# A decoder layer's projections: TensorE in program order, gates deferred, x in natural order, bias repeats pinned, value stores merged

## The chip, the cores and the metric

The kernel runs on one core of a Trainium2 chip, in one launch. The metric is the device time of that launch in microseconds; lower is better. The engines are TensorE (PE, with its weight loads as PEld), VectorE (DVE), ScalarE (ACT), GpSimd (POOL) and SyncE (SP), which mostly issues transfers. ACT issues transfers too; "SPq" and "ACTq" in the profile are the two sequencers at that work.

## What is computed

One layer of a causal decoder on x of 2048 tokens by 1024 columns, all in float32:

```python
nx   = rmsnorm(h, attn_norm_g)
proj = nx @ w_in          # 1024 x 3088: gq gk gv gr glow dq dk dv
glog = log_sigmoid(glow @ gla_gate_w2 + gla_gate_b) / 16
o_a  = gla_mixer(gq, gk, gv, glog)   # chunked gated linear attention, 4 heads
o_a  = rmsnorm_per_head(o_a) * gla_norm_g * silu(gr)
o_b  = dilated_mixer(dq, dk, dv, rel_bias)  # 8 heads, 3 dilations 1, 4, 16
h    = h + concat(o_a, o_b) @ w_out
h    = h + square(relu(rmsnorm(h) @ w_ff1)) @ w_ff2
y    = rmsnorm(h)
```

The change touches the first stage alone: the norm of x, its transposes, the product with `w_in`, the gate, and the rows of biases that the dilated attention reads later.

## The kernel before

Every product in float32 precision is made of three (`mm3`, L66 to L69): the operands are split into a high part (ACT, `split` L345 for x, `prep` L202 for weights) and a rest (DVE, L346, L204, L206). On top of that the projections save an eighth of the products by a block scheme with seven products for eight (`order = (1, 2, 5, 6, 3, 4, 7)`): tokens are halved into tiles 0 to 3 and 4 to 7 (a half of the sequence is eight tiles of 128), the contraction is halved, and the columns of a group are halved.

The work is a list of 126 jobs: two halves of the sequence, nine column groups (`dv gr dq dk dq dk gq gk gv`) and seven products each. `prep(at + 2)` makes the weights of the job after next; `product(at, i)` runs PE and returns `rest`, which combines the result on DVE, ACT and POOL (L302 to L321) and calls `finish` where a block is complete. Jobs of 256 or 264 columns have four products, one for each tile; jobs of 128 columns have one. `finish` stores what is done. For `gr` (jobs 7 to 13 and 70 to 76) it makes silu by way of `log_sigmoid` (L125 to L128: Abs, Exp, Ln on ACT, one operation on DVE), another Exp (L260) and two multiplications (L261, L262), and the last 16 columns, `glow`, go to `gate` (L222 to L233): a transpose on PE (L227), a copy on DVE (L228), a product (L230), `log_sigmoid` and a store. Both PE results lie in PSUM banks with the tag "d", of which there are two. The job that completes `gr` does so for two tiles at a time (blocks 21 and 22), so eight gates arise in its four products.

x of the first half of the sequence is loaded, normed and transposed in the block ahead of the loop (`x_load`, `x_stat`, `x_scale`, `first_half`). That block is a manual schedule: PE, DVE, ACT and POOL take their instructions in program order. x of the second half goes through a generator, `second_half`, one step at each job listed in `OTHER` (7, 9, 10, 11, 12, then 14, 18, 21, 22, 23 and so on every 14): load, norm, two steps of transposes (L378), sums and stores to `nTD`. `reload` brings these back for the second half. Tokens are permuted in all transposed tiles: `token_rows` has partition 8r + i hold token 16i + r, so that 16 tokens of one residue lie side by side.

Behind the first block (jobs 5 and on) nothing is in program order: a scheduler, which times each instruction with a model of its own, orders what every engine issues, PE too. Where the real times differ, an engine waits in the order that was fixed.

`bias_rows` (job 65) computes a row of biases for each head and dilation and stores it to `rowD`; `spread_bias` (L338 to L342), called at every third job from 71 on, has ACT issue a transfer that repeats such rows over 128 partitions into `rbD`, for two heads at a time, twelve times in all.

Of the kernel before, what the change touches and what calls it, by code (L numbers as in the profile page):

```python
# [18 lines left out]
D = 1024  # L19
# [22 lines left out]
def emit(tc, a, stop=99):  # L42
# [34 lines left out]
    ident = const.tile([128, 128], F32, name="ident")  # L77
    make_identity(nc, ident)
    mhalf = const.tile([128, 4], F32, name="mhalf")
    V.memset(mhalf, -0.5)  # L80
    stats = const.tile([128, 96], F32, name="stats")
    stat_at = [0]

    def stat(n=1):
        if stat_at[0] + n > 96:
            stat_at[0] = 0
        s = stats[:, stat_at[0]:stat_at[0] + n]
        stat_at[0] += n
        return s
# [132 lines left out]
    def gate(glow, t):  # L222

        gT = gTs[t % 2]
        V.memset(gT, 1.0)
        pt = ps("d")
        T.transpose(pt[:16, :128], glow, ident)  # L227
        V.tensor_copy(gT[:16], pt[:16, :128])  # L228
        pg = ps("d")[:, :256]
        T.matmul(pg, gT, w2b, start=True, stop=True)  # L230
        e = stage()[:, :256]
        log_sigmoid(e, pg)
        SP.dma_start(glD[t * 128:t * 128 + 128], e)  # L233

    def finish(g, n, k, i):
# [32 lines left out]
        q = SP if g == 0 else A  # L268
        q.dma_start((vD if kind == "dv" else gvD)[tk, j:j + w], s)
        if kind == "dv":  # L270
            q.dma_start(token_rows(vN[:, j:], t, 512, w), s)

    banks = [0]

    def product(at, i):
# [7 lines left out]
        if w == 128:  # L283
            n = 512
            for c in range(4):
                mm3(p, W[0][:, c], W[1][:, c], B[0][:, c], B[1][:, c], c == 0, c == 3)
        else:
            p = p[:, :w]
            tk = slice(i * 128, i * 128 + 128)
            for c in range(4):  # L290
                mm3(p, B[0][:, c, tk], B[1][:, c, tk], W[0][:, c], W[1][:, c], c == 0, c == 3)

        def rest():
# [31 lines left out]
    def bias_rows():  # L325
# [4 lines left out]
        V.tensor_scalar(rb[:32], rb[:32], -1.0, None, op0=OP.mult)  # L330
        SP.dma_start(oh, a["c_onehot"])
        for d in range(3):
            p = ps("o")
# [4 lines left out]
    def spread_bias(d, h):  # L338

        row = rowD[h:, d]  # L340
        A.dma_start(rbD[d][h:h + 2].rearrange("h p n -> p h n"),
                    bass.AP(tensor=row.tensor, offset=row.offset, ap=[[0, 128], [3 * 384, 2], [1, 384]]))  # L342

# [4 lines left out]
    def x_load(t, dst):  # L348
        SP.dma_start(dst, token_rows(x2, t, D))

# [20 lines left out]

    def transposed(xt, last=None):
        out = []
        for q in range(2):
            pv = view(ps("cd"[q]), (4, 128))
            for k in range(4):
                of = xt[:, (4 * q + k) * 128:(4 * q + k + 1) * 128]
                T.transpose(pv[:, k, :], last if last is not None and 4 * q + k == 7 else of, ident)  # L378
            out.append(pv)
# [5 lines left out]
    def first_half(t):  # L385

        pv = transposed(xs[t])
        i = t % 4
# [21 lines left out]
    def second_half():  # L410

        b = [view(bp[:, 512 * q:], (4, 128)) for q in range(4)]
        for i in range(4):
# [10 lines left out]
            for k in range(2):  # L424
                for q, pv in enumerate(transposed(xp[:, D * k:])):
                    A.activation(b[2 * k + q], pv, AF.Copy)
# [15 lines left out]
    with tc.manual_schedule(engines={nc.tensor.engine, nc.vector.engine, nc.scalar.engine, nc.gpsimd.engine}):  # L442
        x_load(0, xs[0])
        SP.dma_start(gB, bcast_row(a["attn_norm_g"], D))
        load_w(0, 0, 0)
# [53 lines left out]
    prep(6)  # L499
    other, back = second_half(), []  # L500
    for at in range(5, len(jobs)):
        g = jobs[at][0]
# [10 lines left out]
        if at in OTHER:  # L513
            next(other)
        if at == 7 * NG + 2:
            bias_rows()
        if 7 * NG + 8 <= at < 7 * NG + 44 and at % 3 == 0:
            spread_bias(2 - (at - 7 * NG - 8) // 12, (at - 7 * NG - 8) // 3 % 4 * 2)
    if stop <= 1:
        es.close()  # L520
# [871 lines left out]
```

## Time and profile before

| | |
|---|---|
| median of 3 runs | 2400.09 us (2397.44 to 2403.56) |
| the profiled execution | 2398.99 us, span 2397.2 us |
| mean granted TensorE clock | 0.985 |
| PE busy | 2306.6 us (96%) |
| DVE, ACT, POOL busy | 1561.9, 1148.0, 583.3 us (65%, 48%, 24%) |
| chain that ended last | PE 77%, DMA 8%, DVE 7%, issue 3%, ACT 3% |
| DMA | 458.13 MB, mean 191 GB/s |

The projections take the first 582 us, the attentions go on to about 960 us, and the rest is the output projection and the MLP. PE is busy almost throughout, but its matmuls are pipelined and their ends are modelled, so the times at which it stood idle tell more than the share. A "granted clock" below 1.00 means that for part of the stretch PE ran at half speed. A wait line reads: who waited, for whom, us in total, times, longest.

### The profile page before, as it was taken

The page shows a single profiled execution, that of the slowest core. Times are in us where ns is not written, and L with a number is a line of the kernel's source. Part 1 is how long each engine was busy: PE and PEld are TensorE (multiplying, and loading weights), DVE is VectorE, ACT ScalarE, POOL GpSimd, SP SyncE. Part 2 cuts the span into 40 slices and gives each one's busy share as a digit, 9 for nine tenths or more (in the row PEclk, how much of TensorE's full clock was granted, in tenths as well). Part 3 has the DMA queues.
Part 4 walks back from the last instruction along what each step waited for, and adds up shares of the span by engine and source line. Part 5 has one row for each costly group of instructions (what it writes and reads, how often), then busy time and mean ns, then how long its engine had stood idle before and what let it go on. Part 6 is the DMA issues. An engine that isn't in the chain of part 4 may idle for free.

```text
span 2397.2 us, 35124 instructions
## 1 busy us (share of the span) xinstructions
PE 2306.6 (96%) x12648; PEld 1989.9 (83%) x12648; DVE 1561.9 (65%) x2879; ACT 1148.0 (48%) x2181; POOL 583.3 (24%) x551
## 2 busy tenths in 40 slices
PE   6999998999999989999999999999999999999998
PEld 5877898779989988888788887888888888888886
DVE  6878666765667668445677778877773455556555
ACT  5565434533767657223455556555563333224323
POOL 5555435446566665100000000000000100001002
PEclk9999999999999999999999999999999999999999
DMA  6457664757888867468664447544467496457653
GB/s 159 120 164 230 213 189 136 206 166 194 213 193 226 225 174 241 154 201 267 203 206 145 145 149 242 176 162 157 155 203 274 155 315 208 168 170 248 217 167 106
DMA packets 342540, 458.13 MB, mean 191 GB/s; under 512 B 19620, under 2 KB 215733, under 8 KB 336094
## 3 DMA queue, kind: packets, MB, share of 16 engines
q1 hardware_dynamic: 313614, 413.15, 56.0%
q10 hardware_dynamic: 28752, 42.74, 5.2%
q8 instruction: 99, 1.62, 0.3%
q14 instruction: 75, 0.61, 0.1%
HBM read 293.51 MB, written 167.02 MB: 192 GB/s over the span
## 4 chain that ended last, share of the span: by engine, by line
PE 77%; DMA 8%; DVE 7%; issue 3%; ACT 3%; POOL 1%; SPq 1%; ACTq 0%; POOLq 0%; DVEq 0%
PE ps_a L67 8%; PE ps_a L68 8%; PE ps_a L69 8%; PE ps_c L67 7%; PE ps_c L69 7%; PE ps_c L68 7%; PE ps_d L67 4%; PE ps_d L69 4%; PE ps_d L68 4%; PE ps_a L672 4%; PE ps_o L67 3%; PE ps_o L68 3%; PE ps_o L69 3%; PE ps_d L653 2%; DMA cmb<-boD 2%
## 5 line engine op out<-in xcount | busy, mean ns | idle before, releaser
L1226 POOL TENSOR_TENSOR suma<-suma,gs 128x512 f32<-128x512 f32 x16 | 23.3, 1472 | 1152.6 <-ACT scr L1224 1152.5
L346 DVE TENSOR_TENSOR ca<-ra,ca 128x1024 fp32r<-128x1024 f32 x112 | 137.7, 1230 | 164.4 <-ACT ca L345 164.4
L345 ACT ACTIVATE ca<-ra 128x1024 fp32r<-128x1024 f32 x112 | 118.0, 1054 | 225.8 <-PE ps_c L69 185.4
L345 ACT ACTIVATE w1comb<-w1raw 128x512 fp32r<-128x512 f32 x224 | 139.6, 627 | 158.7 <-PE ps_c L69 57.7
L644 ACT ACTIVATE pe<-pe,O 128x256 f32<-128x256 f32 (+1 forms) x384 | 157.6, 454 | 89.1 <-DVE O L643 76.3
L672 PE MATMUL ps_a<-v,pt 128*128 128x65 f32 x1200 | 185.1, 258 | 13.3 <-DVE pt L662 8.5
L672 PEld LDWEIGHTS ps_a<-v,pt 128*128 128x128 f32 x1200 | 180.9, 200 | 16.1 <-DVE pt L662 9.5
L346 DVE TENSOR_TENSOR w1comb<-w1raw,w1comb 128x512 fp32r<-128x512 f32 x224 | 153.6, 689 | 53.4 <-ACT w1comb L345 53.2
L653 PE MATMUL ps_d<-ident,pe 128*128 128x128 f32 x600 | 160.9, 284 | 0.0
L643 DVE CUSTOM_DVE_ANT_0 pe<-ps_c,nb 128x256 f32<-128x256 f32 (+1 forms) x384 | 126.6, 360 | 43.4 <-PE ps_d L653 20.6
L204 DVE TENSOR_TENSOR wcomb<-wraw,wcomb 128x512 fp32r<-128x512 f32 (+2 forms) x84 | 101.2, 1210 | 70.3 <-ACT wcomb L202 68.8
L202 ACT ACTIVATE wcomb<-wraw 128x512 fp32r<-128x512 f32 (+2 forms) x126 | 96.3, 773 | 103.7 <-PE ps_a L69 20.8
L345 ACT ACTIVATE cb<-rb 128x1024 fp32r<-128x1024 f32 x56 | 59.4, 1061 | 158.0 <-PE ps_o L68 108.1
L67 PE MATMUL ps_c<-hb,w1comb 128*128 128x512 f32 x336 | 132.2, 393 | 2.8 <-ACT hb L345 2.8
L68 PE MATMUL ps_c<-hb,w1comb 128*128 128x512 f32 x336 | 132.2, 393 | 1.6 <-DVE w1comb L346 1.6
L69 PE MATMUL ps_c<-hb,w1comb 128*128 128x512 f32 x336 | 131.8, 392 | 0.0
L67 PE MATMUL ps_c<-cb,ca 128*128 128x512 f32 x336 | 130.8, 389 | 0.0
L68 PE MATMUL ps_c<-cb,ca 128*128 128x512 f32 x336 | 130.8, 389 | 0.0
L69 PE MATMUL ps_c<-cb,ca 128*128 128x512 f32 x336 | 130.8, 389 | 0.0
L653 PEld LDWEIGHTS ps_d<-ident,pe 128*128 128x128 f32 x600 | 111.1, 190 | 0.4
L94 POOL TENSOR_TENSOR stats<-stats,mhalf 128x1 f32<-128x1 f32 (+1 forms) x64 | 46.4, 730 | 259.3 <-DVE stats L93 216.1
L346 DVE TENSOR_TENSOR cb<-rb,cb 128x1024 fp32r<-128x1024 f32 x56 | 68.2, 1221 | 62.5 <-ACT cb L345 62.3
(351 smaller groups left out, 7330.2 us busy)
## 6 DMA issues: line engine op xcount, KB each, us to landing
ra<-actD SPq DMA_DIRECT2D x56, 1024.0 KB, 6.8
actD<-acc SPq DMA_DIRECT2D x192, 256.0 KB, 2.3
rb<-w_ff SPq DMA_DIRECT2D x72, 512.0 KB, 4.8
w1raw<-w_ff SPq DMA_DIRECT2D x32, 1024.0 KB, 7.3
k<-kD SPq DMA_DIRECT2D x32, 512.0 KB, 11.5
rb<-hTD SPq DMA_DIRECT2D x14, 1024.0 KB, 5.9
wraw<-w_in SPq DMA_DIRECT2D x48, 256.0 KB, 3.4
boD<-O SPq DMA_DIRECT2D x8, 1056.0 KB, 6.2
```

Of the source, the lines that this page charges most:

```text
L67: T.matmul(out, sh, mh, start=first, stop=False)
L68: T.matmul(out, sl, mh, start=False, stop=False)
L69: T.matmul(out, sh, ml, start=False, stop=last)
L94: G.tensor_tensor(r2, r, mhalf[:, :n], op=OP.pow)
L202: A.activation(hi, src, AF.Copy, scale=sc)
L204: V.tensor_tensor(lo, src, hi.bitcast(F32), op=OP.subtract)
L345: A.activation(hi, src, AF.Copy)
L346: V.tensor_tensor(lo, src, hi.bitcast(F32), op=OP.subtract)
L643: V.tensor_tensor_reduce(p, s, bias, scale=1.0, scalar=BIG, op0=OP.add, op1=OP.min, accum_out=nm)
L644: A.activation(p, p, AF.Exp, bias=nm, scale=-1.0)
L653: T.transpose(pb[:, i * 128:i * 128 + 128], src, ident)
L672: T.matmul(self.b.opsum[:, n % 4], self.pt[:, i * 128:i * 128 + 128], self.b.v[:, blk, cols], start=first, stop=last)
```

## The change

Six edits:

- The loop over jobs 5 to 125 is put under a manual schedule for TensorE alone: PE's instructions keep program order, those of the other engines are still ordered by the scheduler.
- `gate` is cut in two. Its transpose is put in a list `waiting` that the next `product` empties behind its own matmuls; the transpose puts the gate's product in the list for the product after that. The two buffers `gTs` alternate by block of four tiles in place of by tile.
- `x_load` reads 128 consecutive tokens in natural order. The permutation goes into the transposes: they take a matrix `perm` in place of `ident` (made on POOL at the start). The ring of statistics is cut from 96 to 48 columns.
- The gain `gB` is no longer loaded with a transfer that repeats its row over 128 partitions: one row is loaded by ACT's queue and spread by two products with a row of ones, which ACT copies out of PSUM. ACT does both copies ahead of its first statistic of x.
- Values (`dv`, `gv`) are stored to `vD` and `gvD` once for four tiles; the stores of `vN` stay one for each tile.
- `bias_rows` is begun at job 63 (loads) and continued at job 66 (products); each transfer of `spread_bias` is pinned behind what ACT was given before it in the program.

```diff
--- before.py
+++ after.py
@@ -76,13 +76,18 @@
     A.preload_act_table_set("natural_log_exp_and_others")
     ident = const.tile([128, 128], F32, name="ident")
     make_identity(nc, ident)
+
+    perm = const.tile([128, 128], F32, name="perm")
+    G.memset(perm, 0.0)
+    G.affine_select(out=perm, in_=perm, compare_op=OP.not_equal, fill=1.0, base=0, pattern=[[-1, 16], [-16, 8]],
+                    channel_multiplier=1)
     mhalf = const.tile([128, 4], F32, name="mhalf")
     V.memset(mhalf, -0.5)
-    stats = const.tile([128, 96], F32, name="stats")
+    stats = const.tile([128, 48], F32, name="stats")
     stat_at = [0]
 
     def stat(n=1):
-        if stat_at[0] + n > 96:
+        if stat_at[0] + n > 48:
             stat_at[0] = 0
         s = stats[:, stat_at[0]:stat_at[0] + n]
         stat_at[0] += n
@@ -221,16 +226,23 @@
 
     def gate(glow, t):
 
-        gT = gTs[t % 2]
-        V.memset(gT, 1.0)
-        pt = ps("d")
-        T.transpose(pt[:16, :128], glow, ident)
-        V.tensor_copy(gT[:16], pt[:16, :128])
-        pg = ps("d")[:, :256]
-        T.matmul(pg, gT, w2b, start=True, stop=True)
-        e = stage()[:, :256]
-        log_sigmoid(e, pg)
-        SP.dma_start(glD[t * 128:t * 128 + 128], e)
+        gT = gTs[t // 4 % 2]
+
+        def transpose():
+            V.memset(gT, 1.0)
+            pt = ps("d")
+            T.transpose(pt[:16, :128], glow, ident)
+            V.tensor_copy(gT[:16], pt[:16, :128])
+            waiting.append(rest)
+
+        def rest():
+            pg = ps("d")[:, :256]
+            T.matmul(pg, gT, w2b, start=True, stop=True)
+            e = stage()[:, :256]
+            log_sigmoid(e, pg)
+            SP.dma_start(glD[t * 128:t * 128 + 128], e)
+
+        waiting.append(transpose)
 
     def finish(g, n, k, i):
 
@@ -266,11 +278,13 @@
             return
         j = n * w
         q = SP if g == 0 else A
-        q.dma_start((vD if kind == "dv" else gvD)[tk, j:j + w], s)
         if kind == "dv":
             q.dma_start(token_rows(vN[:, j:], t, 512, w), s)
-
-    banks = [0]
+        if i == 3:
+            q.dma_start((vD if kind == "dv" else gvD)[512 * tb:512 * tb + 512, j:j + w].rearrange("(i p) n -> p i n", i=4),
+                        c[:, :4 * w].rearrange("p (i n) -> p i n", i=4))
+
+    banks, waiting = [0], []
 
     def product(at, i):
 
@@ -289,6 +303,9 @@
             tk = slice(i * 128, i * 128 + 128)
             for c in range(4):
                 mm3(p, B[0][:, c, tk], B[1][:, c, tk], W[0][:, c], W[1][:, c], c == 0, c == 3)
+        now, waiting[:] = waiting[:], []
+        for f in now:
+            f()
 
         def rest():
             X, c11, c12, c21, c22 = [v[:, i * n:i * n + n] for v in (CX, *C[0], *C[1])]
@@ -329,6 +346,7 @@
         V.memset(rb[32:33], NEG)
         V.tensor_scalar(rb[:32], rb[:32], -1.0, None, op0=OP.mult)
         SP.dma_start(oh, a["c_onehot"])
+        yield
         for d in range(3):
             p = ps("o")
             T.matmul(p[:8, :384], rb, oh[:, d], start=True, stop=True)
@@ -338,15 +356,16 @@
     def spread_bias(d, h):
 
         row = rowD[h:, d]
-        A.dma_start(rbD[d][h:h + 2].rearrange("h p n -> p h n"),
-                    bass.AP(tensor=row.tensor, offset=row.offset, ap=[[0, 128], [3 * 384, 2], [1, 384]]))
+        tc.keep_in_program_order(A.dma_start(
+            rbD[d][h:h + 2].rearrange("h p n -> p h n"),
+            bass.AP(tensor=row.tensor, offset=row.offset, ap=[[0, 128], [3 * 384, 2], [1, 384]])))
 
     def split(hi, lo, src):
         A.activation(hi, src, AF.Copy)
         V.tensor_tensor(lo, src, hi.bitcast(F32), op=OP.subtract)
 
     def x_load(t, dst):
-        SP.dma_start(dst, token_rows(x2, t, D))
+        SP.dma_start(dst, x2[t * 128:t * 128 + 128])
 
     X = {}
 
@@ -369,13 +388,13 @@
         for cs in (slice(0, 512), slice(512, D)) if t == 0 else (slice(0, D),):
             V.scalar_tensor_tensor(xs[t][:, cs], x_src(t)[:, cs], X[t], gB[:, cs], op0=OP.mult, op1=OP.mult)
 
-    def transposed(xt, last=None):
+    def transposed(xt, last=None, by=ident):
         out = []
         for q in range(2):
             pv = view(ps("cd"[q]), (4, 128))
             for k in range(4):
                 of = xt[:, (4 * q + k) * 128:(4 * q + k + 1) * 128]
-                T.transpose(pv[:, k, :], last if last is not None and 4 * q + k == 7 else of, ident)
+                T.transpose(pv[:, k, :], last if last is not None and 4 * q + k == 7 else of, by)
             out.append(pv)
         return out
 
@@ -384,7 +403,7 @@
 
     def first_half(t):
 
-        pv = transposed(xs[t])
+        pv = transposed(xs[t], by=perm)
         i = t % 4
         b11, b21 = [view(xs[i][:, 512 * q:], (4, 128)) for q in range(2)]
         if t < 4:
@@ -422,7 +441,7 @@
                 V.scalar_tensor_tensor(xt, xt, r, gB, op0=OP.mult, op1=OP.mult)
             yield
             for k in range(2):
-                for q, pv in enumerate(transposed(xp[:, D * k:])):
+                for q, pv in enumerate(transposed(xp[:, D * k:], by=perm)):
                     A.activation(b[2 * k + q], pv, AF.Copy)
                 yield
             (b11, b21, b12, b22), (t2, t4, t3) = b, [view(xp[:, 512 * q:], (4, 128)) for q in range(3)]
@@ -441,7 +460,13 @@
 
     with tc.manual_schedule(engines={nc.tensor.engine, nc.vector.engine, nc.scalar.engine, nc.gpsimd.engine}):
         x_load(0, xs[0])
-        SP.dma_start(gB, bcast_row(a["attn_norm_g"], D))
+        g1, one = c11[:1, :D], CX[:1, :128]
+        A.dma_start(g1, a["attn_norm_g"])
+        V.memset(one, 1.0)
+        for q in range(2):
+            p = ps("a")
+            T.matmul(p, one, g1[:, 512 * q:512 * q + 512], start=True, stop=True)
+            A.activation(gB[:, 512 * q:512 * q + 512], p, AF.Copy)
         load_w(0, 0, 0)
         x_load(1, xs[1])
         load_w(0, 0, 1)
@@ -497,8 +522,9 @@
         for i in range(4):
             last_sums(i)
     prep(6)
-    other, back = second_half(), []
-    for at in range(5, len(jobs)):
+    other, back, rows = second_half(), [], bias_rows()
+
+    def job(at):
         g = jobs[at][0]
         if at + 2 > 6:
             prep(at + 2)
@@ -512,10 +538,14 @@
                 back.append(reload(order[at + 2 - 7 * NG + 7]))
         if at in OTHER:
             next(other)
-        if at == 7 * NG + 2:
-            bias_rows()
+        if at in (7 * NG, 7 * NG + 3):
+            next(rows, None)
         if 7 * NG + 8 <= at < 7 * NG + 44 and at % 3 == 0:
             spread_bias(2 - (at - 7 * NG - 8) // 12, (at - 7 * NG - 8) // 3 % 4 * 2)
+
+    with tc.manual_schedule(engines={nc.tensor.engine}):
+        for at in range(5, len(jobs)):
+            job(at)
     if stop <= 1:
         es.close()
         return
```

## The prediction

> **What bounds the kernel now.** The page gives TensorE (PE) 96% of the span and 77% of the chain that ended last, so a change pays only where PE stands idle or runs at half clock. The change edits the projections alone, so I read busy time by stretches there first (columns: busy us and count of each engine, then granted PE clock, DMA share, GB/s).
>
> ```profile
> core 0: us, PE busy (x) PEld busy (x) DVE busy (x) ACT busy (x) POOL busy (x), PEclk, DMA share, GB/s
> 0.00:60.00 60.00, 37.80 (x235) 34.56 (x236) 38.42 (x51) 32.48 (x55) 30.75 (x26) 0.91 0.61 159
> ...
> 124.00:148.00 24.00, 21.49 (x108) 16.73 (x106) 19.39 (x32) 14.48 (x35) 14.92 (x15) 0.93 0.41 116
> 148.00:192.00 44.00, 42.93 (x185) 31.74 (x186) 33.82 (x60) 27.99 (x62) 21.30 (x17) 1.00 0.60 184
> 195.00:245.00 50.00, 45.08 (x204) 36.73 (x203) 39.93 (x49) 24.86 (x45) 26.36 (x17) 0.97 0.82 238
> 360.00:395.00 35.00, 27.61 (x208) 26.83 (x206) 18.85 (x22) 13.57 (x31) 15.23 (x10) 0.90 0.62 179
> 407.00:434.00 27.00, 27.00 (x141) 21.61 (x140) 23.45 (x43) 19.59 (x51) 16.96 (x17) 1.00 0.37 109
> 434.00:470.00 36.00, 33.93 (x142) 24.49 (x141) 24.36 (x41) 19.36 (x39) 17.24 (x12) 1.00 0.69 196
> ```
>
> PE idles 22.2 us of the first 60. In eight stretches that cover 60 to 560 it idles 31.6 us more, and three of them grant 0.97, 0.97 and 0.94, so half clock takes 60 x (0.03 + 0.03 + 0.06) = 7.2 us. About 39 us past 60 us is all that an order of PE can win. Next, who ended PE's waits from 60 to 565 us (us in total, times, longest):
>
> ```profile
> PE ps_o L67 <- ACT acc L315: 5.8, 1, 5.8
> ...
> PE ps_c L378 <- DVE stats L93: 2.7, 1, 2.7
> PE ps_d L378 <- DVE stats L93: 2.1, 1, 2.1
> ```
>
> The first is one event, at 362 us. ACT's timeline shows why:
>
> ```profile
> 349.26 1.92 ACTq L341 DMA_DIRECT2D rbD<-rowD  x3
> 351.31 1.46 ACTq L341 DMA_DIRECT2D rbD<-rowD  x2
> ...
> 360.57 3.68 ACTq L341 DMA_DIRECT2D rbD<-rowD  x2
> ...
> 367.54 0.38 ACT L315 ACTIVATE acc<-ps_o 128x256 f32<-128x256 f32 x1 [11.79 <-DMA rbD<-rowD]
> ```
>
> The program spreads twelve bias repeats over 36 jobs; all twelve were issued between 349 and 379 us. They jam ACT's queue, and an eviction stuck behind them holds a bank that PE needs. The other two waits are transposes of x at 211 and 237 us, whose loads were issued late.
>
> The start, ACT's timeline:
>
> ```profile
> 5.86 1.06 ACT L358 ACTIVATE tb<-xp 128x1024 fp32r<-128x1024 f32 x1 [3.86 <-DMA xp<-x]
> ...
> 23.50 1.06 ACT L358 ACTIVATE tb<-acc 128x1024 fp32r<-128x1024 f32 x1 [4.26 <-DMA acc<-x]
> ```
>
> ACT runs in program order there, and everything behind the statistic of x tile 4 stands until 23.50 us. Last, how the DMA engines read x: tokens 16 rows apart at 204 to 209.5 us (first line: packets, MB, share), and a mixed stretch with x in natural order at 941 to 945.5 us:
>
> ```profile
> q1 hardware_dynamic: 234, 0.89, 64.8%
> ```
> ```profile
> q1 hardware_dynamic: 644, 1.63, 99.7%
> ```
>
> That is 16 x 5.5 x 0.648 / 0.89 = 64 engine-us per MB against 16 x 4.5 x 0.997 / 1.63 = 44: the 64 KB pitch is dear. A tile of 0.52 MB takes 2.1 us of all engines so, 1.4 in natural order.
>
> **The start.** Five x tiles save 5 x 0.7 = 3.3 us by tile 4, and the broadcast of the gain (0.52 MB) leaves the queue, 1.4 to 2.1 us: tile 4 lands near 18.4. But ACT gets a tiny load and two copies ahead of x_stat(0). The load takes between 1.3 us (rel_bias, the small load in the chain) and 5.1 (the first x tile, issued 0.72); each product of 512 columns twice the 0.69 us of the 256-column pair at L230, and twice that at half clock; the copies 0.58. The gain is then ready between 6 and 11.5 us; I take 8.5 for a landing of 7.02, so ACT is 2.6 us late at 5.86. It has 4.26 us idle ahead of 23.50 and 1.8 and 0.4 us more waits on x before it, which the faster loads remove: it reaches tile 4 near 23.5 - 6.4 + 2.6 = 19.7, later than the landing. The chain behind it is DVE and POOL work of the same size. Of these 3.8 us I take -3, bounds -6 and +3.
>
> The Trainium skill ("DMA: Bandwidth & Descriptors", Latency and other measured facts) lists slow row pitches from 512 KiB up; 64 KiB is not in its list. Were its list all, natural order would bring nothing, and the gain's queue time alone would give -1.8 here and 2387 in all.
>
> **Bias repeats.** Pinned behind the job that issues them, the twelve go out every third job, over 71 to 107, when rowD has long been written. The event costs the wait of 5.8 us and half clock, 35 x 0.10 = 3.5: -9.3. The issues (0.6 us each) stay on ACT, ahead of evictions, one per 8 to 18 us of PE work; bounds 0 to +3, taken 0, since ACT is busy 58.3 of the 120 us from 420 to 540. Merged stores of values turn each four issues on ACT or SP into one; nothing on PE waits for them once the jam is gone, so 0. The last store of gv lands later, 512 KB as hD's 3.3 us for 2.2, read far into the next stage: 0. Bias rows start two jobs earlier with their products at job 66 as before; PE idles 2.9 us from 300 to 360, of which I give back 1.
>
> **x of the second half.** In the scheduler's order set 2's last transposes ran near 190 and 195 us, nine jobs after their place (jobs counted by their matmuls), so xp was free late, the loads of set 3 went out at 203.56 and PE waited at 211 and again for set 4 at 237. In program order they stand at jobs 21 and 22; set 3's loads at job 28 and transposes at 35 leave 19 us for 8. The two waits, 4.8 us, and 0.03 x 50 = 1.5 of clock go: -6.3. If ACT and DVE still reach the norms late, half stays. Permuting transposes have ident's shape, 0.27 us each: 0. The mask for them on POOL, 0.5 us, is ready by 2 us, first use 8.69. Halving the ring of statistics reuses a column after 16 norms, long read: 0, else one pow of 0.7 us.
>
> **Gates: the cost.** Before, eight gates per half trickled over about 17 jobs, because PE ran ahead and took one when its operand came: one transpose at 129.59 was copied at 134.32, one at 135.50 at 143.88. That cost 2.5 us idle and 0.07 x 24 = 1.7 of clock, 1.1, 0 and 2.1 in the four gate stretches above: 7.4. Now PE must do a token tile's two gate products and the next's two transposes between two products. Both kinds take turns on two banks "d", and a product's bank is free only after Abs, Exp and Ln on ACT and one operation on DVE: 0.37 + 0.41 + 0.41 + 0.41 = 1.6 us at best. So each round of transposes waits for the gate before it, with all later products queued behind on PE. Up to the last transposes ACT owes 8 x 4 silu operations (12.7 us by groups), 6 x 3 gate operations (7.2) and two preps (1.2): 21.1, some 10% less as neighbours overlap. PE has three products of 1.46 (12 matmuls at 0.122), two of 2.72 (12 at 0.227), six gate products at 0.69 and eight transposes at 0.11: 14.8. PE waits 19 - 14.8, near 5 us per half. Bounds: 0, if ACT takes gates first; 20, if all four rounds go like the copy at 143.88. Two stretches tell what that does to the clock:
>
> ```profile
> 136.00:139.50 3.50, 1.72 (x7) 0.88 (x6) 3.39 (x6) 3.47 (x9) 3.07 (x4) 1.00 0.12 41
> 139.50:142.90 3.40, 3.40 (x9) 2.62 (x9) 3.40 (x4) 2.32 (x7) 3.40 (x3) 0.50 0.28 73
> ```
>
> A stretch half busy was followed by one at half clock. So one such stretch per half, 1.7 us each. Sum: 2 x 5 + 2 x 1.7 - 7.4 = +6.0.
>
> The Trainium skill ("TensorE: Matmul & The Clock Gate", Part 1) wants a whole idle window of some 3.4 us before the clock halves; the trace disagrees, with 1.72 us busy of 3.50. By the page the clock's 3.4 us would be absent.
>
> **The sum.** -3 - 9.3 - 1 - 6.3 + 6.0 = -13.6 on the profiled execution's 2398.99 us (span 2397.2): 2385.4. The median of three runs stands 1.1 above that execution, so 2386.
>
> **Rivals.** *Gates free:* if ACT and DVE keep up, the +6.0 turns into -7.4, and of PE's waits on fresh weights (L202, L204, L206: 8.5 us in the list of waits) 5 go as ACT's queue clears: 2368. For it: ACT is only 54 to 73% busy in the gate stretches. Against: DVE is 68 to 87% busy there. *Gates stall PE, slower:* each of the eight rounds waits 5 us, clock included, as a copy that comes 8.4 us after its transpose would make it: 40 - 7.4 = +32.6 for the gates' +6.0, and +13 in sum: 2413. It decides from (19.6 + 7.4) / 8 = 3.4 us per round; I reckon (10 + 3.4) / 8 = 1.7. For it: DVE's queue stood 2.7 us for x up to 134.25, and a PE in order now stands behind that too. Against: once ACT and DVE hold PE back, they stop falling behind. *Nothing in sum:* all engines but PE are ordered anew by the scheduler, and a new late eviction in the projections or the attention behind them costs what the jam did, 9 to 13 us: 2397. That the edits don't act is not to be had for PE's order; for the repeats, the pin leaves them free to sit later, never earlier.
>
> **Numbers.** Forecast 0.55, gates free 0.14, nothing 0.13, gates stall 0.18. 0.3%, 7.2 us, is about what a measurement here can tell from no change. Faster takes the forecast but 0.04, and gates free: 0.65; same: 0.13 + 0.04 = 0.17; slower 0.18. The range goes from the gates-free case to just short of the stalled one: 2368 to 2408; the forecast's own is 2376 to 2396.
>
> **What would show it.** Right: x tile 4's statistic at 19 to 21 us; L341 issues at least 8 us apart and no wait of 5 us at 360; no wait on L93 at 211 or 237; gate products (L230's successor) within five jobs instead of seventeen, with a few PE waits there on ACT or DVE of 1 to 2 us. Wrong: gate waits over 3.4 us a round with clock at half, ACT's first statistic later than 11 us with nothing won at 23, or new waits of PE past 560 us, where I expect the chain unchanged.

## The result, and the profile after

The changed kernel takes 2421.93 us (median of four runs, 2420.24 to 2425.3), the kernel before 2398.84 beside it: a ratio of 1.0099, 95% interval 1.0081 to 1.0117. It is slower by some 23 us, where 13 less were forecast. The profiled execution took 2420.84 us (span 2419.0, clock 0.982).

A table by jobs places it. A job starts at its first matmul, counted in each trace; columns are stretches of the profiled executions in us.

| | to job 5 | 5–13 | 13–21 (gates) | 21–31 | 31–63 | 63–70 | 70–76 | 76–91 (gates) | 91 to attention | attentions | rest |
|---|---|---|---|---|---|---|---|---|---|---|---|
| before | 70.6 | 53.6 | 34.4 | 33.4 | 122.8 | 46.9 | 45.3 | 52.6 | 122.3 | 375.2 | 1440.1 |
| after | 66.8 | 54.0 | 54.1 | 35.8 | 126.0 | 46.1 | 36.0 | 67.2 | 123.8 | 367.5 | 1441.6 |

The two gate stretches cost 19.7 and 14.6 us more, 34.3 in all, where +6.0 was forecast. The bias stretch gives the 9.3 that were forecast, the start 3.8. Jobs 31 to 63, where x of the second half was to give 6.3, are 3.2 longer, and jobs 21 to 31 are 2.4 longer. The attentions, which the change does not touch, are 7.7 us shorter in this profile and hide part of the loss.

PE's waits from 60 to 600 us in the changed kernel, the first two of the list (us in total, times, longest):

```profile
PE ps_d L234 <- DVE acc L133: 23.1, 6, 8.8
PE ps_a L67 <- ACT wcomb L207: 8.0, 4, 3.2
```

L234 is the gate's transpose (L227 before), L133 the last operation of log-sigmoid (L128 before): PE waits for the bank that the gate before holds. The single bias event on L315 (5.8 us) and the waits on L93 are gone. Windows from the start of job 13 to that of job 17 and from job 76 to job 80 show both halves of the price, waits and clock, first after, then before (busy us and count, then clock, DMA share, GB/s):

```profile
120.80:164.10 43.30, 25.92 (x111) 19.79 (x110) 26.63 (x61) 25.05 (x68) 15.75 (x18) 0.76 0.32 99
418.80:454.20 35.40, 26.29 (x110) 19.95 (x109) 21.26 (x52) 22.10 (x64) 15.11 (x16) 0.76 0.28 83
```
```profile
407.00:422.00 15.00, 15.00 (x91) 12.93 (x89) 12.08 (x21) 10.21 (x28) 10.25 (x11) 1.00 0.21 63
124.20:143.20 19.00, 17.22 (x90) 14.04 (x89) 14.39 (x25) 10.84 (x26) 11.49 (x12) 0.91 0.48 133
```

The two stretches take 78.7 us instead of 34.0, 44.7 more. PE now idles 17.4 and 9.1 us, against 1.8 and 0: 24.7 more. Its busy time rose from 32.2 to 52.2 us. At full clock its work there is 2 x (48 x 0.122 + 36 x 0.227) = 28.1 us for the products and, by the timeline's rows below, 2 x (16 x 1.13 / 4 + 8 x 0.39 / 2) = 12.2 for all gates, 40.3 in all: some 12 us are half clock. The rest of the rise are gates that the kernel before ran later, in jobs 17 to 21 and 80 to 91. Those jobs take 15.4 and 37.6 us before, 10.8 and 31.8 after, which gives 10.4 of the 44.7 back.

PE's timeline in the first gate stretch gives the rounds (start, us, then the idle time before it and who ended it):

```profile
125.38 0.39 PE L234 MATMUL ps_d<-ident,acc 128*16 128x128 f32 x2 [1.49 <-POOL acc L335]
127.15 1.13 PE L240 MATMUL ps_d<-misc 17*128 17x256 f32 x4
137.06 0.37 PE L234 MATMUL ps_d<-ident,acc 128*16 128x128 f32 x1 [8.78 <-DVE acc L133]
...
140.75 1.52 PE L240 MATMUL ps_d<-misc 17*128 17x256 f32 x4
145.47 0.37 PE L234 MATMUL ps_d<-ident,acc 128*16 128x128 f32 x1 [3.19 <-DVE acc L133]
```

After the gate products at 127.15 PE stands 8.78 us for the bank, after those at 140.75 another 3.19. ACT's timeline says what it did meanwhile:

```profile
128.32 1.06 ACT L439 ACTIVATE bp<-xp 128x1024 f32<-128x1024 f32 x1 [1.95 <-DMA xp<-x]
...
133.41 0.36 ACT L130 ACTIVATE acc<-ps_d 128x256 f32<-128x256 f32 x1
```

L439 is the norm of x of the second half, a step of job 18 in the program. The scheduler put it, and silu, ahead of the Abs of a gate of job 13, which starts 5 us after the end of its product.

### The profile page after: what moved, and what is told of

Its sections match the earlier page's. It is cut to its first block, busy times and chain, and to the rows that moved or that the text cites. A ratio compares the mean times of both kernels' runs of the same rounds, so it can differ in the third digit from the quotient of the medians.

```text
span 2419.0 us, 35070 instructions
## 1 busy us (share of the span) xinstructions
PE 2313.7 (96%) x12652; PEld 1996.2 (83%) x12652; DVE 1565.9 (65%) x2880; ACT 1148.5 (47%) x2183; POOL 575.8 (24%) x553
## 4 chain that ended last, share of the span: by engine, by line
PE 81%; DVE 7%; DMA 6%; ACT 3%; issue 2%; POOL 1%; ACTq 0%; SPq 0%; POOLq 0%; DVEq 0%
PE ps_a L67 9%; PE ps_a L68 9%; PE ps_a L69 9%; PE ps_c L68 7%; PE ps_c L67 7%; PE ps_c L69 7%; PE ps_d L67 4%; PE ps_d L68 4%; PE ps_d L69 4%; PE ps_a L702 3%; PE ps_o L68 3%; PE ps_o L69 3%; PE ps_o L67 3%; PE ps_d L683 2%; DMA cmb<-boD 2%
## 5 line engine op out<-in xcount | busy, mean ns | idle before, releaser
L702 PE MATMUL ps_a<-v,pt 128*128 128x65 f32 x1200 | 180.1, 254 | 12.5 <-DVE pt L692 9.5
L702 PEld LDWEIGHTS ps_a<-v,pt 128*128 128x128 f32 x1200 | 175.8, 196 | 15.1 <-DVE pt L692 10.3
L207 ACT ACTIVATE wcomb<-wraw 128x512 fp32r<-128x512 f32 (+2 forms) x126 | 96.3, 774 | 148.1 <-PE ps_o L69 20.9
L673 DVE CUSTOM_DVE_ANT_0 pe<-ps_c,nb 128x256 f32<-128x256 f32 (+1 forms) x384 | 126.5, 361 | 39.7 <-PE ps_d L683 15.8
```

The lines of the kernel that those rows point to most:

```text
L207: A.activation(hi, src, AF.Copy, scale=sc)
L673: V.tensor_tensor_reduce(p, s, bias, scale=1.0, scalar=BIG, op0=OP.add, op1=OP.min, accum_out=nm)
L702: T.matmul(self.b.opsum[:, n % 4], self.pt[:, i * 128:i * 128 + 128], self.b.v[:, blk, cols], start=first, stop=last)
```

## Experiments

Each kernel ran beside the kernel before on the same chip; ratios are to that. The median of the kernel before went from 2394.1 to 2398.8 us between chips, so compare ratios, not medians. Stretches and waits are those of one profiled execution of each kernel.

| kernel | median us | ratio (95%) |
|---|---|---|
| after | 2421.9 | 1.0099 (1.0081 to 1.0117) |
| a_unsplit | 2435.1 | 1.0155 (1.0132 to 1.0178) |
| a_silu_short | 2424.3 | 1.0102 (1.0077 to 1.0127) |
| a_gate_copy | 2415.4 | 1.0068 (1.0046 to 1.0090) |
| a_gate_bank | 2412.9 | 1.0063 (1.0044 to 1.0082) |
| a_order_pin | 2408.0 | 1.0063 (1.0044 to 1.0082) |
| a_order_part | 2410.5 | 1.0048 (1.0028 to 1.0067) |
| a_gate_alt | 2409.7 | 1.0047 (1.0029 to 1.0064) |
| a_copy_pin | 2401.3 | 1.0031 (1.0021 to 1.0041) |
| a_gate_own | 2401.0 | 1.0018 (1.0003 to 1.0034) |
| b_pins | 2395.1 | 1.0004 (0.9992 to 1.0016) |
| b_front | 2396.5 | 0.9997 (0.9984 to 1.0009) |
| b_pin | 2394.8 | 0.9988 (0.9978 to 0.9998) |
| a_own_pin | 2394.2 | 0.9986 (0.9973 to 0.9998) |
| a_no_order | 2392.1 | 0.9973 (0.9962 to 0.9984) |
| a_norm_pin | 2384.3 | 0.9941 (0.9923 to 0.9958) |

### Is it PE's order?

**a_no_order**: all edits but the manual schedule.

```diff
-    with tc.manual_schedule(engines={nc.tensor.engine}):
-        for at in range(5, len(jobs)):
-            job(at)
+    for at in range(5, len(jobs)):
+        job(at)
```

> After, without the manual schedule of TensorE over jobs 5 to 125; the split gates, the natural order of x, the pinned repeats and the merged stores stay. Theory (bank): the scheduler again takes a gate's steps when their operands and banks are free, so nothing but the gains is left: before less 3.8 (start) less 9.3 (repeats), about 2386. Rival (the other edits): if x, the gain or the split gates cost the time, it stays above 2405.

Measured: 2392.1, faster than before by 0.27%, some 6.5 us, half of the 13 that the theory gave. The order alone costs 1.0099 - 0.9973 = 1.26%, some 30 us; jobs 13 to 21 take 35.0 us, 76 to 91 take 53.4, and PE's list of waits has none on L133.

**a_unsplit**: the changed kernel with the gate in one piece.

```diff
-            waiting.append(rest)
+            rest()
...
-        waiting.append(transpose)
+        transpose()
```

> After, with the gate in one piece again: its transpose, copy, product and log-sigmoid are traced where the block is finished, in TensorE's program order. Theory (chain): the split hides part of the chain behind one product, and without it each of the sixteen gates shows its transpose's operand, its copy and the bank of the gate before: slower than after by 5 to 30 us, 2427 to 2452. Rival: the split is what costs, since it puts transposes right behind gate products; then it is as after or faster, 2400 to 2422.

Measured: 2435.1, as the theory had it. Splitting the gate is worth 13 us under PE's order, so the split is not what costs.

**a_order_part**: program order on jobs 5 to 12, 19 to 75 and 82 to 125 only.

```diff
+    in_order(5, 13)
+    for at in range(13, 19):
+        job(at)
+    in_order(19, 76)
+    for at in range(76, 82):
+        job(at)
+    in_order(82, len(jobs))
```

> After, with the manual schedule of TensorE over jobs 5 to 12, 19 to 75 and 82 to 125 alone, so that the scheduler places the gates' steps in the six jobs behind each completion of gr. Theory (chain): the loss sits in jobs 13 to 18 and 76 to 81, so nearly all of the 30 us between after and a_no_order goes: 2388 to 2397. Rival (order everywhere): half or more stays, above 2405.

Measured: 2410.5. Jobs 13 to 21 come down to 33.9 us and 76 to 91 to 53.4, so the excess over before in both stretches is gone with the order there. But jobs 21 to 31 take 45.9 instead of 35.8: gate steps that were left over stand in front of the ordered part, and PE waits there for them, 4.6 us on L234 and 2.2 on L240. So the stretch of the gates is where order costs, but 1.0048 - 0.9973 = 0.75% of the 1.26% stays: part of the cost moves on.

### What holds a round?

**a_gate_bank** (the gate's product takes a bank "c") and **a_gate_alt** (transposes and gate products in alternate products) give PE more work between a gate's steps.

```diff
-            pg = ps("d")[:, :256]
+            pg = ps("c")[:, :256]
```

> After, with one word changed: the gate's product takes a PSUM bank with the tag c (three banks) in place of d (two). The order of TensorE is the same. Theory (bank): in program order a gate's transpose waits until the gate product ahead of it has been read by log-sigmoid, because both use the two banks d; the list of waits after names this wait with 23.1 us, and the half clock behind it takes some 15 more (120 to 180 us at 0.83, 420 to 480 at 0.86). Expected: that wait falls under 5 us and the time to 2385 to 2395. Rival (backlog): ACT and DVE owe the silu and gate work anyway, so the wait comes back at the next products (fresh weights, evictions, or the bank of the next gate product) and the time stays at 2412 to 2422.

```diff
-            waiting.append(rest)
+            waiting.insert(0, rest)
...
-        now, waiting[:] = waiting[:], []
+        now, waiting[:] = waiting[:2], waiting[2:]
```

> After, with the gates' two kinds of steps in alternate products: each product runs at most two waiting steps, either two transposes or two gate products, so a whole product of the projections stands between a gate product and the next transpose, and the eight gates of a half take some eight products in place of five. The banks are those of after. Theory (bank): each wait shrinks by the product in between, 1.5 us in the first rounds and 2.7 later, and the half clock goes with it: 2388 to 2402. Rival (backlog): ACT and DVE are as late as before, 2412 to 2422.

Measured: 2412.9 and 2409.7. The time of a_gate_bank is what its rival, the backlog, gave; that of a_gate_alt lies between its two theories. The first line of PE's waits in a_gate_bank:

```profile
PE ps_c L240 <- DVE acc L133: 15.9, 5, 6.7
```

The wait moves from the transpose to the product; in a_gate_alt the transposes still wait 18.5 us, once 10.8. Some 9 to 12 us come back, not the whole. More distance or another bank shortens the waits, but log-sigmoid still ends late.

**a_silu_short**: of silu of gr only one Exp and the multiplications are left, three ACT operations and one of DVE fewer for each of 32 blocks. It leaves out the rest of silu, and only its time is of use.

```diff
-            log_sigmoid(sg, s[:, :m])
-            A.activation(sg, sg, AF.Exp)
+            A.activation(sg, s[:, :m], AF.Exp)
```

> The changed kernel with the silu of gr cut short: of its Abs, Exp, Ln, DVE operation and second Exp only one Exp is left (so s times exp(s) in place of silu); the gates keep their four operations. This takes three of four ACT operations and one of two DVE operations of each of the 32 silu blocks out of the gate stretches and leaves the chain that holds the bank as long as it was. Backlog: the gates' waits fall to under a third (from 23.1 us to under 8) and both stretches shrink by 25 us together: 2395 or less. Chain: the waits stay above 15 us, and only what ACT and DVE otherwise hold up goes, some 5 us: 2416.

Measured: 2424.3, nothing gained; jobs 13 to 21 take 53.7 us, 76 to 91 take 67.0, and PE still waits 15.6 us on L133 beside the 9.1 of the next line. So a backlog of silu, the reason that I had by then taken for the main one, falls. PE's long round stays:

```profile
137.19 0.37 PE L234 MATMUL ps_d<-ident,acc 128*16 128x128 f32 x1 [9.11 <-POOL stats L99]
```

and ACT's timeline shows it standing still, with little to do:

```profile
124.61 0.41 ACT L271 ACTIVATE acc<-acc 128x248 f32<-128x248 f32 x1 [1.62 <-DVE acc L335]
130.41 1.06 ACT L438 ACTIVATE bp<-xp 128x1024 f32<-128x1024 f32 x1 [5.39 <-DMA xp<-x]
...
133.41 0.63 ACT L130 ACTIVATE acc<-ps_d 128x256 f32<-128x256 f32 x2
```

It waits 5.39 us for x (the norm is L438 here), and the gate's Abs is behind that. In this kernel the long round waits for a transfer of x, by way of ACT's queue.

**a_order_pin**: the changed kernel with that norm pinned on ACT behind the program's earlier ACT work.

```diff
-                A.activation(bp[:, :D], xt, AF.Square, accum_out=ss)
+                tc.keep_in_program_order(A.activation(bp[:, :D], xt, AF.Square, accum_out=ss))
```

> The changed kernel, PE's order and gates untouched, with only the square sum of the norm of x of the second half pinned on ACT behind its earlier work. In the changed kernel ACT takes that norm at 128.32 us, ahead of the first gate's Abs at 133.41; with silu cut short it stood 5.39 us for x at 130.41 and PE's 9.1 us wait stayed. Theory 'x in front of gates': the longest round (8.8 us of 23.1) and its clock go, jobs 13 to 21 fall from 54.1 to about 44, jobs 21 to 63 lose what the pin gave the other kernels (7 to 9 us), and the time is 2398 to 2408. Rival: the rounds are the serial chain transpose, copy, product, log-sigmoid alone; then only the 7 to 9 us of jobs 21 to 63 go and jobs 13 to 21 stay above 50: 2412 to 2416.

Measured: 2408.0; 1.0099 - 1.0063 is 0.36%, some 9 us. The long round is halved:

```profile
133.11 0.62 PE L234 MATMUL ps_d<-ident,acc 128*16 128x128 f32 x2 [4.35 <-DVE acc L133]
```

Jobs 13 to 21 take 47.4 us, between the two theories; jobs 31 to 63 take 122.2 instead of 126.0. So x in front of the gates was half of the longest round; the rounds behind it stay. In the second half of the sequence, where no norm of x is left to do, the first round waits 4.2 us with and without the pin. But PE now waits for the transposes of x, whose norms come later:

```profile
PE ps_c L397 <- DVE xp L441: 7.3, 4, 2.9
```

**a_gate_copy** and **a_copy_pin**: one DVE operation copies the gate's product out of its bank, and log-sigmoid works on the copy; the second kernel has the pin too.

```diff
-            e = stage()[:, :256]
-            log_sigmoid(e, pg)
+            z, e = stage()[:, :256], stage()[:, :256]
+            V.tensor_copy(z, pg)
+            log_sigmoid(e, z)
```

> The changed kernel, but each gate product is first copied out of its bank by one DVE operation, and Abs, Exp, Ln and the DVE operation of log_sigmoid work on the copy; the bank is free after one operation. One more DVE operation of about 0.4 us per gate, 16 in all. Theory 'chain': what PE waits for is the length of the chain of four operations over two engines that holds the bank. Then the waits of the gate's transposes on the log-sigmoid's DVE operation (23.1 us, 6 times, longest 8.8 in the changed kernel) fall below 8, both gate stretches (54.1 and 67.2 us for jobs 13 to 21 and 76 to 91) shrink by some 22 us together, and the time falls to about 2400. Theory 'backlog': ACT and DVE serve silu and the norms of x first, and whatever operation frees the bank comes late. Then the copy is as late as the Abs was, the waits go over to the copy with at least two thirds of their length, and the time stays above 2413.

> The same with the gate products copied out of their bank by one DVE operation, as in the run with the copy alone (2415.4 us, where one wait of 8.5 us was left of the gates' 23.1). If that one was x and the rest the bank, gate waits fall below 6 us in all, jobs 13 to 21 take 36 to 40 us, and the time is 2392 to 2398. If the two causes overlap, it is within 3 us of the run with the pin alone.

Measured: 2415.4 and 2401.3. In a_gate_copy the gates' main wait goes from six times to two, but one of them is 8.5 us, so the time is that of the theory 'backlog'. With the pin that wait is gone and no gate waits over 2.3 us, so it was the norm of x. First a_gate_copy, then a_copy_pin:

```profile
PE ps_d L234 <- DVE acc L242: 10.7, 2, 8.5
...
PE ps_d L234 <- DVE misc L235: 3.3, 4, 1.2
```
```profile
PE ps_d L234 <- DVE misc L235: 5.5, 4, 1.9
PE ps_d L234 <- DVE acc L242: 4.5, 2, 2.3
PE ps_d L234 <- DVE misc L232: 3.3, 4, 1.7
```

Both causes are real and add up: the copy is worth some 7.5 us by ratio, without the pin and with it (0.31% and 0.32%). But a_copy_pin missed its own forecast, 2392 to 2398, since the waits move on: to the copy of the transpose (L235) and to the memset of its buffer (L232). They are 13.3 us in all, where under 6 was expected. Jobs 13 to 21 take 42.7 us, 76 to 91 still 63.2.

A round of the changed kernel is a trip from PE (transpose) to DVE (copy), PE (gate's product), ACT (Abs, Exp, Ln), DVE and back to PE, and PE in order has only one product of the projections between two of its own steps. One round of the second half, without a norm in it, by the timelines of PE, ACT and DVE:

```profile
442.27 1.12 PE L240 MATMUL ps_d<-misc 17*128 17x256 f32 x4
443.73 0.64 ACT L130 ACTIVATE acc<-ps_d 128x256 f32<-128x256 f32 x2
444.26 0.72 ACT L131 ACTIVATE acc<-acc 128x256 f32<-128x256 f32 x2
444.87 0.72 ACT L132 ACTIVATE acc<-acc 128x256 f32<-128x256 f32 x2
445.31 0.76 DVE L133 SCALAR_TENSOR_TENSOR acc<-ps_d,acc 128x256 f32<-128x256 f32 x2 [0.76 <-ACT acc L132]
445.88 0.62 PE L234 MATMUL ps_d<-ident,acc 128*16 128x128 f32 x2 [2.49 <-DVE acc L133]
```

Just before it ACT had stood idle for 4.2 us and DVE for 4.1. But for one split of weights on ACT (0.61 us from 443.22) there was no backlog: nearly all of the 2.49 us are the legs themselves.

### What of the order is left without rounds?

**a_gate_own**: eight buffers for transposed gates (four partition groups by two, with a copy of the gate's weights in each group), all eight transposes first, then one gate product per product from job 17 on. **a_own_pin** adds the pin of the norm.

```diff
-        gT = gTs[t // 4 % 2]
+        gT, w2 = gTs[t % 8], w2b[t % 4]
...
-            waiting.append(rest)
+            late.append(rest)
...
+        if late and at % (7 * NG) >= 17:
+            late.pop(0)()
```

> After, with the order of TensorE kept over all jobs, but the gates taken out of its way: eight operand buffers gT in place of two (four partition blocks by two columns), all transposes one product on as in after, and the eight gate products kept back until job 17 of a half, then one for each product. So no transpose follows a gate product, and each of the two banks d has two products of 2.7 us for its log-sigmoid. Theory (chain: the order costs only because TensorE must follow the gates' log-sigmoid chain through ACT and DVE; the runs with another bank and with alternate steps showed the wait moving to the next step of that chain, 15.9 and 18.5 us): the waits at L234 and at the gate product's line (L240 in after) fall under 5 us and the time to that of a_no_order or a little less, 2386 to 2394. Rival (order everywhere): the order costs in other stretches as well, and the time stays above 2400.

> The kernel with PE in program order and eight buffers for the gates' transposes (2401.0 us in its own run), with the same pin on the norm of x as the one without the order. It tells what is left of the order's price once gates no longer stall PE: jobs 21 to 31 took 41.7 us in it against 34.4 without the order, where transposes of x stand in PE's queue. If the early norm of ACT is at the bottom of that (weights of the next jobs split late while ACT stands for x), jobs 21 to 31 come down to 36 and the time to about 2395. The rival: PE in order stands behind transposes whose x is normed late whatever ACT does first; then the pin makes the norms later still, jobs 21 to 31 stay at 41 or more, and the time stays at 2401 or above.

Measured: 2401.0, then 2394.2. With the rounds taken apart, jobs 13 to 21 take 36.2 us in the first, and some 20 of the 30 us that the order costs come back. The time is still that of the rival, above 2400. Jobs 21 to 31 take 41.7, and 38.3 with the pin, neither of the two numbers that the theories gave, though the time with the pin is the theory's. Against a_norm_pin below, PE's order still costs 0.9986 - 0.9941 = 0.45%, 11 us. Its first waits are on gates (6.1 us, none in a_norm_pin) and on transposes of x (5.1, against 3.7). That rest was not taken further apart.

### The other terms

**b_pin**: the kernel before, with only the bias repeats pinned. **b_front**: with only x in natural order, the shorter ring of statistics and the gain through PE (the diff of the change, its parts for `perm`, `stats`, `x_load` and `gB`).

```diff
-        A.dma_start(rbD[d][h:h + 2].rearrange("h p n -> p h n"),
...
+        tc.keep_in_program_order(A.dma_start(
+            rbD[d][h:h + 2].rearrange("h p n -> p h n"),
```

> Before, with one edit of the change alone: each repeat of the biases is pinned behind what ACT was given ahead of it. The prediction's term says -9.3 us: 2387 to 2393 with before at 2399. Rival: the issues only move the jam to other places, or the scheduler's new order takes the gain: 2396 to 2402.

> Before, with the x edits alone: x in natural order, the permutation in the transposes, the ring of statistics at 48 columns, the gain through TensorE. Theory: the first block is 3.8 us shorter as in after, and the four later loads of x land sooner: 2390 to 2396. Rival: what the start gains is lost between jobs 21 and 63, where after and a_no_order were 5 us slower than before in their traces: 2396 to 2401.

Measured: 2394.8 and 2396.5. The pin takes 7.7 us out of the stretch from job 70 to job 77 of its profile (51.3 to 43.6), but only 3 us (0.5 to 5) of the medians, between term and rival. Its own profile shows a loss of the same size: from job 91 to the attention it takes 130.3 us, against 122.3 before, with PE idle 6.1 us instead of 2.7 and a clock of 0.97 instead of 1.00. Six of the twelve repeats are now issued in this stretch, and it is as long in b_pins (130.2). Whether the repeats cause it was not tried; in the changed kernel the stretch is 123.8. b_front reaches job 5 at 66.0 us in its profile, 4.6 earlier than before; at job 91 0.8 are left, and its time cannot be told from no change.

**a_norm_pin** is a_no_order with the pin of the norm, **b_pins** is b_pin with it (the edit is that of a_order_pin).

> The changed kernel without PE's program order (2392.1 us in its own run, against 2397.8 for the kernel before beside it), and with the square sum of the norm of x of the second half pinned on ACT behind the program's earlier ACT work. Without the pin ACT took it early and stood 9.6 us in five waits for x ahead of it, with the splits of the next weights queued behind; jobs 31 to 63 took 126.5 us in the profile against 122.8 in the kernel before. If that early issue is what ate the gain of x in natural order, ACT's waits for x ahead of the norm fall below 3 us, jobs 31 to 63 take 120 to 123 us and the time is 2386 to 2389. The rival: later norms only make the transposes of x late, PE waits on them in place of the weights, and the time stays within 3 us of 2392.

> The kernel before with the pinned bias repeats (2394.8 us in its own run) and the pinned norm of x of the second half, and nothing else. The best version so far (no PE order, both pins, all other edits) took 2384.3. If the pin of the norm works by itself, this takes 2385 to 2389, and the rest of the change is worth at most 3 us. If it works only with x in natural order, with loads short enough to follow the pinned norm, it stays at 2392 or above.

Measured: 2384.3 and 2395.1. ACT's idle time ahead of the norm that x ended (us, times), in a_no_order and in a_norm_pin:

```profile
  DMA xp<-x: 9.6, 5
```
```profile
  DMA xp<-x: 4.2, 1
```

In a_norm_pin jobs 31 to 63 take 121.3 us instead of 126.5, and the time falls by 0.32%, 8 us; one wait of 4.2 us is left where under 3 was expected. In b_pins the same wait falls from 14.2 us (6 times, in the kernel before) to 3.9, but it gains nothing on b_pin, and jobs 21 to 31 take 39.5 us there instead of 33.4: the pin of the norm pays only beside the change's other edits. Which of them (x in natural order, the stores, the split gate) was not tried singly. a_norm_pin beats both kernels: 14 us under before, and 0.9941 / 1.0099, 1.6% under after.

## Why the prediction was wrong

**Right: the start.** ACT's statistics of x tiles 0 and 4:

```profile
7.46 1.05 ACT L377 ACTIVATE tb<-xp 128x1024 fp32r<-128x1024 f32 x1
...
18.21 1.06 ACT L377 ACTIVATE tb<-acc 128x1024 fp32r<-128x1024 f32 x1
```

They were put at 8.5 and 19.7, and ACT was ready 1.0 and 1.5 us sooner; job 5 starts 3.8 us earlier for the -3. b_front shows that such a lead does not last by itself: of 4.6 us at job 5, 0.8 are left at job 91.

**Right in place: the bias repeats.** 9.3 us left jobs 70 to 76, the sum of the step to the tenth, and the repeats now go out apart, on ACT's queue. Two of the twelve:

```profile
402.69 0.59 ACTq L359 DMA_DIRECT2D rbD<-rowD  x1
...
453.24 0.56 ACTq L359 DMA_DIRECT2D rbD<-rowD  x1
```

They lie 5.7 to 34 us apart, where at least 8 was the sign. That the -9.3 came to the tenth is in part luck: by itself the edit is worth 3 us of the medians, a third of the term, and b_pin's profile loses 8 us behind job 91, for a cause that no run took apart. The bias rows' -1 came as -0.8 (jobs 63 to 70), which no run took apart.

**Wrong: the gates, +6.0.** The mechanism was named (transposes wait for the bank that log-sigmoid holds, all later products behind), and the stated point of decision, 3.4 us a round, was passed: with the 7.4 us that the gates cost before, (34.3 + 7.4) / 8 = 5.2 us a round, the price of the rival "gates stall PE". The step that failed is the wait "near 5 us per half". It was had by adding up ACT's work until the last transposes, 19 us, and taking off PE's 14.8, as if ACT were busy without a break and took gates in turn. It was neither. ACT stood for x, for DVE and for PE. The first round's 8.78 us had a norm of job 18 in it, on ACT and then on DVE, and half of the round went with the pin. And a round is a trip whose legs add up even where every engine is half idle: with silu cut short, ACT busy 23.3 of the 60 us from 120 to 180, it did not get shorter. PE idles 17.4 and 9.1 us in place of 5 and 5.

The second half of the failed term is the clock: two windows at 1.7 us each, 3.4, were reckoned, and some 12 were paid. Granted 0.76, the two stretches ran 2 x 0.24 x 78.7 = 38 us at half clock, part of it idle, where two windows of 3.5 were allowed. One such passage, by stretches:

```profile
443.40:445.88 2.48, 0.00 (x0) 0.03 (x1) 1.43 (x4) 2.19 (x8) 1.18 (x1) 0.90 0.00 0
445.50:448.80 3.30, 2.92 (x8) 2.26 (x9) 1.10 (x4) 0.09 (x1) 0.46 (x1) 0.50 0.27 83
```

PE idles 2.48 us and then runs 3.3 us at half clock, so that round costs 2.5 + 1.6 us. A mean of 0.90 in the idle stretch means that the clock fell 0.10 x 2.48 / 0.50 = 0.5 us before its end, 2.0 us after PE had gone idle. The same holds at 153.26 to 155.74 us, again 2.48 us idle at 0.90 with 0.50 behind it. The Trainium skill ("TensorE: Matmul & The Clock Gate", Part 1) has the clock halve after an idle window of some 3.4 us; by the page, rounds under 3.4 us would have cost no clock. The trace disagrees, with 2.48 us.

**Wrong: x of the second half, -6.3.** Natural order reads as cheaply as reckoned; the load queue from 196 to 203 us (packets, MB, share):

```profile
q1 hardware_dynamic: 457, 1.11, 41.9%
q10 hardware_dynamic: 288, 0.52, 19.6%
```

That is 16 x 7.0 x 0.419 / 1.11 = 42 engine-us per MB, against 64 at the 64 KB pitch and the 44 reckoned. The other queue, q10, moved its bytes at 42 as well, and at 45 in the prediction's window at 204 to 209.5 us of the kernel before, so the traffic beside it does not make the difference:

```profile
q10 hardware_dynamic: 243, 0.43, 22.0%
```

The list of slow pitches in the Trainium skill ("DMA: Bandwidth & Descriptors", Latency and other measured facts) begins at 512 KiB; here 64 KB is slow too. What failed is "the two waits go". PE's order fixed PE's place of the transposes, not ACT's of the norms:

```profile
200.88 1.06 ACT L439 ACTIVATE bp<-xp 128x1024 f32<-128x1024 f32 x1 [5.20 <-DMA xp<-x]
...
203.88 0.61 ACT L207 ACTIVATE wcomb<-wraw 128x512 fp32r<-128x512 f32 x1
...
204.54 0.50 PE L67 MATMUL ps_a<-tb,wcomb 128*128 128x512 f32 x1 [3.17 <-ACT wcomb L207]
```

ACT takes the norm early, stands 5.20 us for x, and the split of the next weights comes late behind it: PE waits 3.17 us for L207, the longest of the 8.0 in the list above. The prediction had "if ACT and DVE still reach the norms late"; they came too early. Jobs 21 to 63 take 156.2 us before, 161.8 after and 154.1 in a_order_pin. So the pin takes the excess off and brings 2 of the 6.3 us, not all: there PE waits 7.3 us for transposes of x, where the two waits to be saved were 4.8.

**The attentions** were to stay unchanged, and what they gave is luck; they took 367.5 us instead of 375.2 in this profile, and 367 to 375 among the variants, with no pattern that the edits explain. That stays open.

Two small slips of the prediction change nothing: the stretches from 60 to 560 us are nine, not eight (their 31.6 us of idle time stand), and its "landing of 7.02" for the gain stands in no row; the gain was ready for ACT's first statistic at 7.46 us, where 8.5 was taken.

## What to carry to other kernels

To put one engine in program order while others are ordered by a scheduler fixes who waits, not for what: before doing it, look at what the other engines have queued ahead of the operation that frees its bank, above all anything that waits for a transfer. Price a round trip between engines by adding up its legs, not by the busy time of the engines in it, and add to each wait of PE the half clock that follows. Where a scheduler brings forward an operation that waits for a transfer, try to pin that one operation in its place: that gave 8 us here, beside the change's other edits, and nothing in the kernel before, while ordering the engine that suffered from it cost some 30.

## What the runs showed of the hardware

A PE idle time of 2.48 us was followed by 3.3 us at half clock, so this wait cost PE some 1.6 us more than it lasted. Reading x at a 64 KB pitch took 64 engine-us per MB, in natural order 42. In the two gate stretches, some 12 us of half clock came on top of 26.5 us of idle time.
